# Transposes of two attention steps side by side in every second step

## The chip, the cores and the metric

The kernel runs on one core of a Trainium2 chip. The time is the device time of one execution in microseconds; the number compared is the median over runs. The core's engines run side by side, each through its own list of instructions in order: TensorE (PE in the profile; PEld is its loading of weights), VectorE (DVE), ScalarE (ACT), GpSimd (POOL, hardly used here) and SyncE (SP), which issues the DMAs.

## What is computed

Two layers of an encoder on 512 tokens of 1024 channels. In each layer four token mixers work on one projected input, are gated and summed; an MLP follows. The change touches two of the four, A and C, which have eight query heads and two key and value heads each, of 64 channels. Cut to what matters:

```python
def mixer_a(q, k, v, ...):        # dense: every token sees every token
    sc = einsum('bqhgd,bkhd->bhgqk', qblk, k) * hd ** -0.5
    p = softmax(sc, axis=-1)
    return einsum('bhgqk,bkhd->bqhgd', p, v)

def mixer_c(q, k, v, sink, ...):  # banded: |i - j| <= 128, with a sink logit per head
    sc = where(abs(rel) <= 128, einsum(...) * hd ** -0.5, NEG_INF)
    m = maximum(max(sc, axis=-1), sink)
    p = exp(sc - m)
    l = sum(p) + exp(sink - m)
    o = einsum(p, v) / l
```

## The kernel before

Each matrix is split into a high and a low part (`whi`, `wlo` for weights, `xh`, `xl` for activations), and a product is made of three matmuls per 128 rows, high by high, high by low, low by high (lines 177 to 179). ScalarE makes the high part by a cast (`whi`, L118), VectorE the low part by a subtraction (`wlo`, L127). Weights come by DMA three blocks ahead.

Attention A and then attention C of a layer run through `attn_gqa`. The 512 queries of a head are four tiles of 128, the quarters; a head and a quarter are a **step**, numbered 0 to 31 in an attention (step k is head k//4, quarter k%4). In A a step has four key blocks of 128; in C, where the window is narrow, quarters 0 to 3 have two, three, three and two. The parts of a step, named by a letter:

- `s` scores: two matmuls into a PSUM tile `ps_s` (L796, L797). Two buffers.
- `e` exps: the row's maximum on VectorE (L806 in A, L812 in C), the exponential into `P` on ScalarE (L808 with the sum read after it; L820 and L822 in C). `P` has four buffers.
- `n` norm: the reciprocal of the sum on VectorE (L828), `P` scaled by it on ScalarE (L829).
- `t` transposes: one transpose on TensorE for each key block, from `P` into a PSUM tile `ps_t` (L835). Two buffers.
- `h` high: ScalarE casts `ps_t` into the high half of `PT` (L842). `PT` of a head has one buffer, so the next head's first `h` waits for the values matmuls of the head before.
- `l` low: VectorE subtracts (L845) and by that releases `ps_t`.
- `v` values, only in the fourth quarter: eight matmuls with the transposed probabilities of the whole head (L856); then `o`, `p`, `q` add up and split the output (L863 to L874).

`pipeline` sets the order by hand. It goes through rounds; in round i every entry of a table `ORD` is taken in turn, and an entry such as `t3` means part t of step i - 3. What is written first in a round stands first on its engine. A has the order `v5 t3 h4 n2 e1 o6 l4 s0 q8 p7`; C has `h4 v5 n2 e1 l4 q8 s0 t3 o6 p7`, so its transposes stand at the end of the round, behind the scores. A step's transposes thus stand one round ahead of its `h` and `l`.

`merge` puts other matmul work between the rounds, the **fill**: in A the gates and the projection of mixer B, in C the value projection of mixer D (matmuls of 256 columns, with `vst` copies on ScalarE, L688) and the gates and projection of A. One or two pieces of six matmuls of 512 columns, or twelve of 256, stand between two rounds. The fill's weights are cast on ScalarE and VectorE in the same queues in which the attention's work stands, and its results are taken up there too (L719 to L727).

Of the kernel before, what the change touches and what calls it, by code (L numbers as in the profile page):

```python
# [34 lines left out]

ORD = [[(w[0], int(w[1:])) for w in o.split()] for o in (
    "v5 t3 h4 n2 e1 o6 l4 s0 q8 p7",
    "h4 v5 n2 e1 l4 q8 s0 t3 o6 p7",
)]

MG = ((35, 48, 3), (41, 71, 2), (18, 47, 12))
# [34 lines left out]
class Body:  # L76
# [687 lines left out]
    def attn_gqa(self, l, which, y):  # L764

        nc, ap = self.nc, self.ap
        nv, ns = nc.vector, nc.scalar
        isA = which == 0
        qs = self.qsA if isA else self.qsC
        Kt, Qt, PT, YT = {}, {}, {}, {}  # L770

        def blocks(i):
            return (0, 4) if isA else (max(0, i - 1), min(4, i + 2))
# [11 lines left out]
        def step(h, i):  # L785
            j = h // 4
            b0, b1 = blocks(i)
            n = (b1 - b0) * 128
            st = {}

            def scores():
                if i == 0 and h + 3 < 8:
                    load_q(h + 3)
                ps = st["s"] = self.ps("s")
                qq = Qt[h][:, i * 128:(i + 1) * 128]
                nc.tensor.matmul(ps[:, 0:n], qq, Kt[j][:, 0, b0 * 128:b1 * 128], start=True, stop=False)  # L796
                nc.tensor.matmul(ps[:, 0:n], qq, Kt[j][:, 1, b0 * 128:b1 * 128], start=False, stop=True)  # L797

            def exps():
                ps = st["s"]  # L800
                P = st["P"] = ap.tile([128, S], F32, tag="P", name="P", bufs=4)
                m, nm, ls = self.smt(1, "am"), self.smt(1, "an"), self.smt(1, "al")
                st["l"] = ls
                if isA:
                    rs = self.rqs[:, i, h:h + 1]
                    nv.tensor_reduce(out=m, in_=ps[:, 0:n], axis=AX.X, op=ALU.max, negate=True)  # L806
                    nv.tensor_tensor(out=nm, in0=m, in1=rs, op=ALU.mult)
                    ns.activation(out=P[:, 0:n], in_=ps[:, 0:n], func=AF.Exp, scale=rs, bias=nm, accum_out=ls)  # L808
                else:
                    rs = self.rs8[:, i:i + 1]  # L810
                    mo = C_MC + (b0 - (i - 1)) * 128
                    nv.tensor_tensor_reduce(  # L812
                        out=P[:, 0:n], in0=ps[:, 0:n], in1=self.cs[:, mo:mo + n], scale=1.0, scalar=-3.0e38,
                        op0=ALU.add, op1=ALU.max, accum_out=m,
# [4 lines left out]
                    )  # L819
                    ns.activation(out=P[:, 0:n], in_=P[:, 0:n], func=AF.Exp, scale=rs, bias=nm, accum_out=ls)  # L820
                    e = st["e"] = self.smt(1, "ae")
                    ns.activation(out=e, in_=nm, func=AF.Exp, bias=self.v(l, V_SINK + h), scale=1.0)  # L822

            def norm():
                P, ls = st["P"], st["l"]
                if not isA:
                    nv.tensor_tensor(out=ls, in0=ls, in1=st["e"], op=ALU.add)
                nv.reciprocal(out=ls, in_=ls)  # L828
                ns.activation(out=P[:, 0:n], in_=P[:, 0:n], func=AF.Copy, scale=ls)  # L829

            def transposes():
                P = st.pop("P")
                pt = st["t"] = self.ps("t")
                for b in range(b1 - b0):
                    nc.tensor.transpose(pt[:, b * 128:(b + 1) * 128], P[:, b * 128:(b + 1) * 128], self.ident)  # L835

            def high():
                if i == 0:
# [33 lines left out]
            def out3():  # L872
                if h % 2 == 1:
                    nv.tensor_tensor(  # L874
                        out=y[:, 1, h // 2], in0=YT[h // 2], in1=y[:, 0, h // 2].bitcast(F32), op=ALU.subtract
                    )

            d = dict(s=scores, e=exps, n=norm, t=transposes, h=high, l=low)
            return d | (dict(v=values, o=out1, p=out2, q=out3) if i == 3 else {})

        load_k(0)
# [2 lines left out]
        load_k(1)  # L884
        yield
        steps = [step(h, i) for h in range(8) for i in range(4)]
        yield from self.pipeline(steps, ORD[0 if isA else 1])

# [593 lines left out]
```

## Time and profile before

| | |
|---|---|
| median of 3 runs | 2031.62 us |
| their range | 2030.08 to 2032.27 us |
| the profiled execution | 2030.6 us |
| its span, first to last instruction | 2028.8 us |
| PE busy in the span | 2008.3 us, 99% |
| DVE busy | 1270.8 us, 63% |
| ACT busy | 974.1 us, 48% |
| DMA, mean of the 16 engines | 112 GB/s |

The profile is of one execution. In a row of a timeline stand the start from the span's first instruction and the duration in us, the engine, the line of the code, the operation, the output and the inputs, the shape and how many are merged; in square brackets stands how long the engine was idle before and what ended that. Matmuls overlap each other, and their ends are modelled, so the distance of their starts tells what one costs. Attention A of layer 1 runs from about 208 to 319 us, C from 321 to 437; in layer 2 they are at 1210 to 1322 and 1323 to 1440.

### The profile page before, as it was taken

Reading aid. Unit: us, or ns where it says so; the run is one execution under the profiler, and the core shown is the slowest. Engines: PE = TensorE matmul, PEld = TensorE weight load, DVE = VectorE, ACT = ScalarE, POOL = GpSimd, SP = SyncE. Lnnn points to the kernel's source line nnn. Section 1 sums busy time; section 2 is a strip of 40 time slices with the busy share of each in tenths; the row PEclk is TensorE's granted clock in tenths of the full one; section 3 lists DMA queues with packets and bytes.
Section 4 is the critical chain, followed back from the end, with each engine's and each line's share of the span. In section 5 each row is a group of like instructions: output and inputs, shape, how many; then the busy total and the mean of one; then the engine's idle time right before and its main releaser. Section 6 shows DMA issues by size and latency. Waiting matters only on the chain.

```text
span 2028.8 us, 25698 instructions
## 1 busy us (share of the span) xinstructions
PE 2008.3 (99%) x9752; PEld 1665.0 (82%) x9752; DVE 1270.8 (63%) x2274; ACT 974.1 (48%) x1701; POOL 0.2 (0%) x4
## 2 busy tenths in 40 slices
PE   9999999999999999999999999999999999999998
PEld 7888789887778888888878888898877888888887
DVE  6889775764466544444658897758644665444445
ACT  4357786854534332322323668868445334322322
POOL 0000000000000000000000000000000000000000
PEclk9999999999999999999999999999999999999998
DMA  5454425332134233223335552152421522323231
GB/s 191 136 158 142 130 67 146 116 125 84 53 114 138 94 102 94 96 94 104 123 105 166 156 166 94 62 160 91 135 73 48 173 94 94 104 94 97 94 100 63
DMA packets 87439, 227.03 MB, mean 112 GB/s; under 512 B 15098, under 2 KB 21370, under 8 KB 87316
## 3 DMA queue, kind: packets, MB, share of 16 engines
q1 hardware_dynamic: 84436, 221.20, 34.5%
q10 hardware_dynamic: 2880, 4.20, 0.6%
q8 instruction: 77, 1.26, 0.3%
q14 instruction: 46, 0.38, 0.1%
HBM read 201.08 MB, written 24.27 MB: 111 GB/s over the span
## 4 chain that ended last, share of the span: by engine, by line
PE 89%; DVE 6%; ACT 2%; issue 1%; DMA 1%; SPq 0%; DVEq 0%; ACTq 0%
PE ps_mm L177 13%; PE ps_mm L178 13%; PE ps_mm L179 13%; PE ps_s L177 6%; PE ps_s L178 6%; PE ps_s L179 6%; PE ps_t L177 6%; PE ps_t L179 6%; PE ps_t L178 6%; PE ps_o L856 2%; PE ps_t L835 2%; PE ps_s L796 1%; PE ps_s L797 1%; DVE tt L338 1%; DVE wlo L127 1%
## 5 line engine op out<-in xcount | busy, mean ns | idle before, releaser
L118 ACT CAST whi<-raw 128x1024 fp32r<-128x1024 f32 (+1 forms) x318 | 329.0, 1041 | 334.9 <-PE ps_mm L178 105.6
L127 DVE TENSOR_TENSOR wlo<-raw,whi 128x1024 fp32r<-128x1024 f32 (+1 forms) x318 | 385.0, 1215 | 98.6 <-ACT whi L118 95.6
L177 PE MATMUL ps_mm<-xh,whi 128*128 128x512 f32 x720 | 289.0, 401 | 0.0
L179 PE MATMUL ps_mm<-xh,wlo 128*128 128x512 f32 x720 | 282.6, 392 | 0.0
L178 PE MATMUL ps_mm<-xl,whi 128*128 128x512 f32 x720 | 282.5, 392 | 0.0
L177 PEld LDWEIGHTS ps_mm<-xh,whi 128*128 128x128 f32 x720 | 136.1, 189 | 32.4 <-issue 4.1
L179 PEld LDWEIGHTS ps_mm<-xh,wlo 128*128 128x128 f32 x720 | 135.9, 189 | 29.8
L178 PEld LDWEIGHTS ps_mm<-xl,whi 128*128 128x128 f32 x720 | 136.2, 189 | 26.7
L177 PE MATMUL ps_t<-xh,whi 128*128 128x512 f32 x368 | 143.7, 390 | 0.0
L178 PE MATMUL ps_t<-xl,whi 128*128 128x512 f32 x368 | 143.3, 389 | 0.0
L179 PE MATMUL ps_t<-xh,wlo 128*128 128x512 f32 x368 | 143.2, 389 | 0.0
L177 PE MATMUL ps_s<-xh,whi 128*128 128x512 f32 x352 | 138.6, 394 | 0.0
L179 PE MATMUL ps_s<-xh,wlo 128*128 128x512 f32 x352 | 137.1, 390 | 0.0
L178 PE MATMUL ps_s<-xl,whi 128*128 128x512 f32 x352 | 137.0, 389 | 0.0
L845 DVE TENSOR_TENSOR PT<-ps_t,PT 128x512 fp32r<-128x512 f32 (+2 forms) x128 | 75.1, 587 | 63.9 <-ACT PT L842 54.7
L829 ACT ACTIVATE P<-P,al 128x512 f32<-128x512 f32 (+2 forms) x128 | 82.6, 645 | 17.0 <-DVE al L828 15.7
L719 DVE TENSOR_TENSOR gt<-ps_mm,rb 128x512 f32<-128x512 f32 x54 | 37.2, 688 | 78.3 <-PE ps_mm L179 77.9
L842 ACT CAST PT<-ps_t 128x512 fp32r<-128x512 f32 (+2 forms) x128 | 63.8, 500 | 46.6 <-PE ps_o L856 43.1
L177 PEld LDWEIGHTS ps_t<-xh,whi 128*128 128x128 f32 x368 | 69.1, 188 | 17.3 <-issue 3.0
L179 PEld LDWEIGHTS ps_t<-xh,wlo 128*128 128x128 f32 x368 | 69.1, 188 | 14.3
L178 PEld LDWEIGHTS ps_t<-xl,whi 128*128 128x128 f32 x368 | 69.1, 188 | 14.2
L177 PEld LDWEIGHTS ps_s<-xh,whi 128*128 128x128 f32 x352 | 66.1, 188 | 14.9 <-issue 1.4
(423 smaller groups left out, 4218.2 us busy)
## 6 DMA issues: line engine op xcount, KB each, us to landing
raw<-in_w_dram SPq DMA_DIRECT2D x314, 512.0 KB, 3.5
qsA<-stk SPq DMA_DIRECT2D x32, 128.0 KB, 2.3
qsC<-stk SPq DMA_DIRECT2D x32, 128.0 KB, 2.3
K<-ks SPq DMA_DIRECT2D x16, 256.0 KB, 6.0
Q<-qsA SPq DMA_DIRECT2D x16, 256.0 KB, 3.8
Q<-qsC SPq DMA_DIRECT2D x16, 256.0 KB, 7.0
qD<-stkf SPq DMA_DIRECT2D x24, 128.0 KB, 2.2
kD<-stkf SPq DMA_DIRECT2D x24, 128.0 KB, 2.2
```

The costliest lines, as they stand in the source:

```text
L118: self.nc.scalar.copy(hi[:, s], self.raws[i][:, s])
L127: self.nc.vector.tensor_tensor(out=lo[:, s], in0=raw[:, s], in1=hi[:, s].bitcast(F32), op=ALU.subtract)
L177: mm(ps, sh, mh, start=(k == 0), stop=False)
L178: mm(ps, sh, ml, start=False, stop=False)
L179: mm(ps, sl, mh, start=False, stop=(k == n - 1))
L338: nv.tensor_tensor(out=o, in0=a, in1=b, op=ALU.mult)
L719: nv.tensor_tensor(out=g, in0=ps, in1=self.rb, op=ALU.mult)
L829: ns.activation(out=P[:, 0:n], in_=P[:, 0:n], func=AF.Copy, scale=ls)
L835: nc.tensor.transpose(pt[:, b * 128:(b + 1) * 128], P[:, b * 128:(b + 1) * 128], self.ident)
L842: ns.copy(st["dst"][0], st["src"])
L845: nv.tensor_tensor(out=st["dst"][1], in0=st["src"], in1=st["dst"][0].bitcast(F32), op=ALU.subtract)
L856: nc.tensor.matmul(o, a, b, start=(n_ == 0), stop=(n_ == len(mm) - 1))
```

## The change

Only odd steps have transposes now, and they transpose the step before as well: eight transposes in A, five in C, into the two buffers of `ps_t`. An even step's transposes therefore stand one round later than they did, in the round of its own `h` and `l`. In C the transposes move from the round's end to its front, and `h` behind them.

```diff
 ORD = [[(w[0], int(w[1:])) for w in o.split()] for o in (
     "v5 t3 h4 n2 e1 o6 l4 s0 q8 p7",
-    "h4 v5 n2 e1 l4 q8 s0 t3 o6 p7",
+    "t3 h4 v5 n2 e1 l4 q8 s0 o6 p7",
 )]
...
+            before = (ST.get((h, i - 1)), (blocks(i - 1)[1] - blocks(i - 1)[0]) * 128) if i % 2 else None
+            ST[h, i] = st
...
             def transposes():
-                P = st.pop("P")
-                pt = st["t"] = self.ps("t")
-                for b in range(b1 - b0):
-                    nc.tensor.transpose(pt[:, b * 128:(b + 1) * 128], P[:, b * 128:(b + 1) * 128], self.ident)
+
+                for sb, w in ((before[0], before[1]), (st, n)):
+                    P = sb.pop("P")
+                    pt = sb["t"] = self.ps("t")
+                    for o in range(0, w, 128):
+                        nc.tensor.transpose(pt[:, o:o + 128], P[:, o:o + 128], self.ident)
...
-            d = dict(s=scores, e=exps, n=norm, t=transposes, h=high, l=low)
+            d = dict(s=scores, e=exps, n=norm, h=high, l=low) | (dict(t=transposes) if i % 2 else {})
```

In the changed file the lines stand two to four further down: scores are L798 and L799, transposes L839, `h` L846, `l` L849, values L860.

TensorE in A, at the end of head 0. Before, with the last values matmul, then two rounds; `P_2152` and `P_2178` are steps 5 and 6:

```order
L856 MATMUL ps_o_2203<-PT1_2080,VV_196 128x512
L835 MATMUL ps_t_2212<-cs_77,P_2152 128x128 x4
L796 MATMUL ps_s_2232<-K_1852,Q_1859 128x512
L797 MATMUL ps_s_2232<-K_1852,Q_1859 128x512
...
L835 MATMUL ps_t_2248<-cs_77,P_2178 128x128 x4
L796 MATMUL ps_s_2267<-K_1852,Q_1859 128x512
L797 MATMUL ps_s_2267<-K_1852,Q_1859 128x512
```

The same two rounds in the change:

```order
L860 MATMUL ps_o_2198<-PT1_2080,VV_196 128x512
L839 MATMUL ps_t_2207<-cs_77,P_2114 128x128 x4
L839 MATMUL ps_t_2212<-cs_77,P_2152 128x128 x4
L798 MATMUL ps_s_2232<-K_1852,Q_1859 128x512
L799 MATMUL ps_s_2232<-K_1852,Q_1859 128x512
...
L798 MATMUL ps_s_2262<-K_1852,Q_1859 128x512
L799 MATMUL ps_s_2262<-K_1852,Q_1859 128x512
```

Step 4 (`P_2114`), transposed a round earlier before, has come behind the values matmuls; the next round begins with its scores.

TensorE at the start of C, rounds 3 and 4, with the first fill matmul of each. Before; `P_3197` and `P_3240` are steps 0 and 1:

```order
L796 MATMUL ps_s_3292<-K_3133,Q_3136 128x256
L797 MATMUL ps_s_3292<-K_3133,Q_3136 128x256
L835 MATMUL ps_t_3295<-cs_77,P_3197 128x128 x2
L177 MATMUL ps_mm_3264<-whi_3068,xh_83 128x256
...
L796 MATMUL ps_s_3328<-K_3133,Q_3138 128x256
L797 MATMUL ps_s_3328<-K_3133,Q_3138 128x256
L835 MATMUL ps_t_3331<-cs_77,P_3240 128x128 x3
L177 MATMUL ps_mm_3349<-whi_3145,xh_83 128x256
```

In the change:

```order
L798 MATMUL ps_s_3292<-K_3133,Q_3136 128x256
L799 MATMUL ps_s_3292<-K_3133,Q_3136 128x256
L177 MATMUL ps_mm_3264<-whi_3063,xh_83 128x256
...
L839 MATMUL ps_t_3307<-cs_77,P_3197 128x128 x2
L839 MATMUL ps_t_3310<-cs_77,P_3240 128x128 x3
L798 MATMUL ps_s_3332<-K_3133,Q_3138 128x256
L799 MATMUL ps_s_3332<-K_3133,Q_3138 128x256
L177 MATMUL ps_mm_3349<-whi_3145,xh_83 128x256
```

Step 0 is transposed behind twelve fill matmuls instead of ahead of them, and step 1 ahead of the scores of step 4 instead of behind them.

ScalarE at the same place, round 4, in the change; before, the same operations stand there in the same order:

```order
L846 CAST PT0_3314<-ps_t_3307 128x2x128
L831 ACTIVATE P_3283<-P_3283,al_3286 128x384
L822 ACTIVATE P_3320,al_3323<-P_3320,an_3322,rs8_191 128x256
L824 ACTIVATE ae_3327<-an_3322,ve_78 128x1
L118 CAST whi_3335<-raw_3066 128x1024
L118 CAST whi_3338<-raw_3148 128x1024
```

Nothing moved here: step 0's `h` stands first and two weight casts behind it. What moved is the place on TensorE of the transposes that it reads.

## Rows read from the trace of the kernel before

**Rows 1.** The page, busy time: us, share of the span, instructions.

```profile
PE 2008.3 (99%) x9752; PEld 1665.0 (82%) x9752; DVE 1270.8 (63%) x2274; ACT 974.1 (48%) x1701; POOL 0.2 (0%) x4
```

**Rows 2.** Busy time by stretch, A of both layers; stretch, length, engines, clock, DMA.

```profile
208.00:319.00 111.00, 108.50 (x539) 89.38 (x538) 83.97 (x175) 89.41 (x165) 0.00 (x0) 1.00 0.32 97
1210.00:1322.00 112.00, 110.65 (x541) 91.11 (x542) 83.86 (x176) 89.39 (x165) 0.00 (x0) 0.98 0.31 97
```

**Rows 3.** Timeline of PE, a round of A: start, duration, line, operation, count.

```profile
255.78 0.60 PE L835 MATMUL ps_t<-cs,P 128*128 128x128 f32 x4
256.14 0.48 PE L796 MATMUL ps_s<-K,Q 128*128 128x512 f32 x1
256.46 0.39 PE L797 MATMUL ps_s<-K,Q 128*128 128x512 f32 x1
256.69 0.40 PE L177 MATMUL ps_mm<-yB,whi 128*128 128x512 f32 x1
```

**Rows 4.** Timelines of PE and ACT, start of C in layer 1.

```profile
331.90 0.38 PE L835 MATMUL ps_t<-cs,P 128*128 128x128 f32 x2
333.54 0.28 PE L796 MATMUL ps_s<-K,Q 128*128 128x256 f32 x1
336.46 0.39 PE L178 MATMUL ps_mm<-wlo,xh 128*128 128x256 f32 x1 [0.64 <-DVE wlo L127]
...
332.31 0.37 ACT L842 CAST PT<-ps_t 128x256 fp32r<-128x256 f32 x1
334.12 1.98 ACT L118 CAST whi<-raw 128x1024 fp32r<-128x1024 f32 x2
```

**Rows 5.** Timelines of PE and ACT in A, first step of head 1.

```profile
235.04 0.60 PE L835 MATMUL ps_t<-cs,P 128*128 128x128 f32 x4
...
235.01 0.59 ACT L842 CAST PT<-ps_t 128x512 fp32r<-128x512 f32 x1 [3.26 <-PE ps_o L856]
```

**Rows 6.** The same timelines, end of head 1's scores' wait.

```profile
241.90 0.61 PE L835 MATMUL ps_t<-cs,P 128*128 128x128 f32 x4
242.43 0.50 PE L796 MATMUL ps_s<-K,Q 128*128 128x512 f32 x1
...
242.18 0.19 ACT L808 ACTIVATION_READ_ACCUMULATOR P<-ps_s,an,rqs 128x1 f32 x1
```

**Rows 7.** Timelines of PE and DVE, values matmuls in A.

```profile
258.07 1.32 PE L856 MATMUL ps_o<-PT,VV 128*128 128x512 f32 x5
...
257.33 0.69 DVE L845 TENSOR_TENSOR PT<-ps_t,PT 128x512 fp32r<-128x512 f32 x1 [0.41 <-ACT PT L842]
```

**Rows 8.** Timelines of PE and ACT, scores of step 23 in A.

```profile
280.83 0.48 PE L796 MATMUL ps_s<-K,Q 128*128 128x512 f32 x1
...
280.37 0.19 ACT L808 ACTIVATION_READ_ACCUMULATOR P<-ps_s,an,rqs 128x1 f32 x1
```

**Rows 9.** Timelines of PE, ACT and DVE, head 6 in A.

```profile
302.86 0.60 PE L835 MATMUL ps_t<-cs,P 128*128 128x128 f32 x4
307.44 0.85 PE L856 MATMUL ps_o<-PT,VV 128*128 128x512 f32 x3
...
301.35 0.59 ACT L842 CAST PT<-ps_t 128x512 fp32r<-128x512 f32 x1
303.92 0.62 ACT L870 CAST yA<-yt 128x512 fp32r<-128x512 f32 x1 [0.46 <-DVE yt L868]
...
306.61 0.69 DVE L845 TENSOR_TENSOR PT<-ps_t,PT 128x512 fp32r<-128x512 f32 x1 [1.15 <-ACT PT L842]
```

**Rows 10.** Timelines of ACT, DVE and PE, head 1 in C.

```profile
347.97 0.37 ACT L842 CAST PT<-ps_t 128x256 fp32r<-128x256 f32 x1 [1.97 <-PE ps_o L856]
...
350.60 2.36 DVE L127 TENSOR_TENSOR wlo<-raw,whi 128x1024 fp32r<-128x1024 f32 x2 [1.80 <-ACT whi L118]
353.79 0.55 DVE L845 TENSOR_TENSOR PT<-ps_t,PT 128x384 fp32r<-128x384 f32 x1
...
354.48 0.41 PE L835 MATMUL ps_t<-cs,P 128*128 128x128 f32 x2 [0.24 <-DVE PT L845]
```

More of the change, by code (lines that the diff above doesn't have):

```diff
@@ L769, in attn_gqa @@
         qs = self.qsA if isA else self.qsC
-        Kt, Qt, PT, YT = {}, {}, {}, {}
+        Kt, Qt, PT, YT, ST = {}, {}, {}, {}, {}
         def blocks(i):
```

## The prediction

> **What bounds the kernel now.** I read the page first: the matmul engine is busy 2008.3 of the 2028.8 us [rows 1]. The two attention stretches of layer 1 were cut out with the busy times by stretch: in attention A of layer 1 the matmul engine works 108.5 of 111 us and ScalarE 89.4; in layer 2 it is 110.7 of 112 and 89.4 [rows 2]. So whatever makes TensorE wait goes onto the time in full, and ScalarE, at 80%, is near enough to make it wait. The same windows hold 165 ScalarE and about 540 matmul records in both layers: what is found in layer 1 I count twice.
>
> Then the timelines of single engines, at the rounds where something is late. By "round" I mean one pass of the pipeline loop, by "step k" head k//4, quarter k%4.
>
> **The change part by part.**
>
> *Transposes side by side.* In A a group of four starts at 255.78, the first score matmul follows at 256.14, the second at 256.46, and a plain 512-column matmul takes 0.23 (256.46 to 256.69) [rows 3]. Four last 0.60 and two 0.38 [rows 3, 4], so they start (0.60 - 0.38)/2 = 0.11 apart. The group costs 0.68 - 0.23 = 0.45 against 4 x 0.11 = 0.44. So a group's border costs some 0.01 to 0.02 us; 128 groups become 64 pairs, and 64 borders go: **-0.8 us**, between -0.6 and -1.3. No instruction is removed. The rest of the change is when things happen.
>
> *What is moved.* An even step's transposes (0.44 in A; 0.22 or 0.33 in C, where a step has two or three) leave their round and stand in the next, in front of the odd step's. The orders of ScalarE and VectorE stay as they were. In that next round stands the even step's high copy (ScalarE, line 842), and ScalarE takes its work in order: so far the transposes were a round old when the copy came up, now they are the newest thing TensorE has done. Behind the copy on ScalarE stand the scaling (L829) and the exponentials (L808, L820) of later steps and the weights' `whi` casts (L118); behind those, on VectorE, `low` (L845) and `wlo` (L127); TensorE waits for all of them. Nothing of SP's queue moves. In A the scores of odd steps also come 0.36 earlier (255.78 to 256.14), since no transposes stand before them, and the values matmuls 0.45 earlier.
>
> *A, first step of a head.* The copy at 235.01 had waited 3.26 for the values matmuls, whose last starts 0.23 before the transposes at 235.04, so 0.20 before the copy [rows 5]. Now four transposes come between: 0.23 + 0.33 to the last of them, and 0.30 from there to the copy (in C the second of two transposes starts at 331.90 + 0.11, the copy at 332.31 [rows 4]); less the 0.20, less the 0.45 by which the values come earlier: the copy is **0.2 late** in every head. ScalarE is then busy without a gap until the exponential that ends at 242.37; the scores at 242.43 were already waiting for it (0.53 after the transposes where 0.36 is usual) [rows 6]. In the change they are ready at 241.90 and wait until about 242.64; the second score matmul starts at 242.87 instead of 242.76, and 0.45 of transposes is still to come: **+0.55**.
>
> *Two smaller ones.* The values matmuls at 258.07 need `low`, which ends at 258.02, for their second instruction at 258.30; they will be ready 0.45 earlier, while `low` comes 0.2 later (the delay of the head's first copy, carried along): 0.65 less the 0.27 of slack, **+0.4** [rows 7]. The scores at 280.83 have 0.27 over an exponential that ends at 280.56; they come 0.36 earlier and it comes 0.2 later: **+0.35** [rows 8].
>
> *A, head 6.* The copy of step 26 ran at 301.35. Its transposes now stand in front of those at 302.86, 0.44 before, so the copy can start at about 302.86 - 0.44 + 0.33 + 0.30 = 303.05, 1.7 later. ScalarE has one gap after it, 0.46 before 303.92, so the next copy (306.02) and `low` (ends 307.30) come about 1.25 late, at 308.55. The values at 307.44 want it for their second instruction, at 307.67 - 0.45: **+1.35** [rows 9].
>
> *C, start.* The copy at 332.31 followed its transposes (331.90) at once. Now these stand in front of the round that begins at 333.54; 0.22 less before it, 0.11 to the second, 0.30 to the copy: 333.73, 1.42 late. Four small ScalarE instructions with about 0.2 of slack stand between it and the two `whi` casts at 334.12; these come 1.2 late, and so does `wlo`, for which TensorE was already waiting (0.64 before 336.46) [rows 4]: **+1.2**.
>
> *C, step 7.* The copy at 347.97 had waited 1.97 for the values; they now stand behind the odd step's three transposes, 0.33 later. ScalarE and then VectorE (from 350.60) run without a gap to `low` of step 5, which ends at 354.34 and releases the buffer for which the transposes at 354.48 had waited. All that comes 0.33 later, and the two score matmuls of 384 columns (0.23 x 384/512 = 0.17 each, an estimate) now stand behind these transposes instead of before them: 0.33 + 0.35 = **+0.65** [rows 10].
>
> *Sum.* A 0.55 + 0.4 + 0.35 + 1.35 = 2.65; C 1.2 + 0.65 = 1.85; 4.5 a layer, 9.0 for both, less 0.8: **+8.2 us**. Against the profiled execution (2030.6, span 2028.8) that is 2038.8; the median of the runs shown is 1.0 above it, 2031.6, and 2039.8 is the forecast. What was not priced: other rounds where slack shrinks below 0.1 (more), and heads in which TensorE, once late, no longer outruns ScalarE (less). I put them at half the sum either way: +4 to +14.
>
> One rule speaks against the change on its own. In the trace the granted clock is 1.00, the 2.4 GHz level, in A of layer 1, with its groups of four transposes, and 0.98 in A of layer 2, with the same groups [rows 2]. The Trainium skill ("TensorE: Matmul & The Clock Gate", Part 4: PE-mode transpose) says that a transpose does not count as activity for the clock as other matmuls do. By it, eight in a row might cost clock where four did not; by the row they don't. The sum goes by the row.
>
> **The rivals.**
> 1. *The late copies are absorbed.* ScalarE waits at the copy, but it is idle 20% of A anyway; if the work behind each late copy has more slack than I read, TensorE never sees it. For it: most rounds are like that, only six places a layer were found. Against: at three of the six TensorE already waits for this very chain [rows 4, 6, 10]. It decides if less than half of each delay arrives. Time: 2031.6 - 0.8 = 2030.8, up to 2035 with a part of the waits. This is the one in which the change is not slower.
> 2. *The waits of today vanish.* TensorE's waits at 242.43 (0.17), 336.46 (0.64 or a little more) and 354.48 (0.24 shown) are all that the change could take away: about 1.2 a layer, 2.4, and the 0.8: 2028.4. Against: each is a wait for ScalarE or VectorE, whose work is not cut. A gain over 4 us has no row to come from.
> 3. *The clock falls during pairs.* In A of layer 2, 0.02 of 112 us, 2.2 us, is what a stretch with a lower grant lost [rows 2]. One such in each of the four stretches: 2039.8 + 9 = 2049. Against: the trace shows 1.00 with half the run length.
> 4. *The kernel as built doesn't do it.* The order of instructions shows pairs and unchanged ScalarE and VectorE; I give it nothing.
>
> **How the numbers follow.** About 0.2%, 4 us, is what a measurement of this kernel can tell from no change: faster is below 2027.6, slower above 2035.7. Forecast 0.64 (of it 0.04 so small that it falls within 0.2%); absorbed 0.27, within 0.2%; waits vanish 0.05 (0.03 faster, 0.02 within); clock 0.04, slower. Faster 0.03, same 0.33, slower 0.64. The likeliest time is 2039.8. The range from 2031.5 to 2046.5 leaves out the lower half of the absorbed case with the vanishing waits, and above it the clock and the worst of the forecast, about 0.2 together. The forecast's own range is 2035 to 2046.
>
> **What would show it.** In the profile after: copies of even steps (line 842 before) that wait for transposes, where they waited for the values matmuls or not at all; a wait of about 1.3 at the values matmuls of head 6 in both layers; the wait before `wlo`'s user at the start of C grown from 0.64 to about 1.9; a group of eight lasting 0.88 without a gap in its middle. Wrong would be: TensorE's sum of waits in the two windows as before (rival 1), a gap inside the pairs, or a granted clock under 1.00 around them (rival 3).

## The result and the profile after

The changed kernel takes 2044.4 us in the median of four runs (2040.9, 2042.3, 2046.5, 2046.5), where the kernel before takes 2031.1 beside it: 1.0069 times as long, 95% interval 1.0053 to 1.0085, so between 10.8 and 17.3 us more. The mean granted clock of the four runs is 0.996, 0.995, 0.994 and 0.994 in the same order. The profiled execution is one of the two long ones: 2046.5 us, span 2044.7, which is 15.9 above the span before.

The page's line of busy time, then the windows of the four attention stretches (stretch, length, busy PE, PEld, DVE, ACT, POOL, granted clock, DMA), which answer to [rows 1, 2]:

```profile
PE 2015.3 (99%) x9752; PEld 1666.7 (82%) x9752; DVE 1270.3 (62%) x2274; ACT 973.0 (48%) x1701; POOL 0.2 (0%) x4
```

```profile
210.00:325.00 115.00, 110.69 (x534) 89.73 (x535) 82.61 (x174) 89.50 (x165) 0.00 (x0) 0.99 0.29 90
327.00:440.00 113.00, 110.44 (x700) 100.02 (x699) 77.67 (x231) 84.10 (x203) 0.00 (x0) 1.00 0.36 114
1220.00:1333.00 113.00, 110.06 (x536) 88.92 (x537) 82.13 (x174) 89.29 (x165) 0.00 (x0) 1.00 0.29 92
1335.00:1449.00 114.00, 111.44 (x698) 101.05 (x697) 77.67 (x231) 84.09 (x203) 0.00 (x0) 0.99 0.35 111
```

ScalarE and VectorE are busy as long as before; TensorE's 9752 instructions, as many as before, are busy 7.0 us longer. The list of what TensorE waited for from A's start to C's end of layer 1 (205 to 440 us), first before, then after (total, times, longest):

```profile
PE ps_s L796 <- DVE btq L652: 2.5, 1, 2.5
PE ps_mm L178 <- DVE wlo L127: 0.6, 1, 0.6
PE ps_t L835 <- DVE PT L845: 0.2, 1, 0.2
```

```profile
PE ps_s L798 <- DMA Q<-qsA: 2.8, 1, 2.8
PE ps_mm L178 <- DVE wlo L127: 1.0, 2, 0.9
PE ps_t L839 <- DVE PT L849: 0.7, 1, 0.7
PE ps_s L798 <- ACT P L810: 0.7, 2, 0.5
PE ps_mm L177 <- ACT whi L118: 0.7, 1, 0.7
PE ps_o L860 <- ACT PT L846: 0.7, 1, 0.7
PE ps_o L860 <- DVE PT L849: 0.4, 2, 0.2
```

Lines of the changed kernel stand 2 (scores, exponentials, scaling) or 4 (transposes, copies, values) lower than before. The first row is the wait at A's very first scores, which both have. All the others are new or longer, and each names ScalarE or VectorE. The rows add up to 3.3 us before and 7.0 after; the loss in this stretch is larger, 5.6 (below), because the end of a matmul is modelled and part of what it waits stands in the profile as busy time.

On the page the group of `high` (busy, mean ns | idle before it) read

```profile
L842 ACT CAST PT<-ps_t 128x512 fp32r<-128x512 f32 (+2 forms) x128 | 63.8, 500 | 46.6 <-PE ps_o L856 43.1
```

and those of `low` and `high` now read

```profile
L849 DVE TENSOR_TENSOR PT<-ps_t,PT 128x512 fp32r<-128x512 f32 (+2 forms) x128 | 75.1, 587 | 78.9 <-ACT PT L846 72.9
L846 ACT CAST PT<-ps_t 128x512 fp32r<-128x512 f32 (+2 forms) x128 | 63.6, 500 | 68.2 <-PE ps_t L839 49.5
```

Before, the copies idled 46.6 us, most of it for the values matmuls; now 68.2, most of it for transposes. But waits of an engine that has slack are no loss.

What is lost is read from the **lag**: the start of a score matmul in the changed kernel less its start before, taken at the even steps' scores, which stand just behind a pair. In A both kernels have done the same work there: where the lag is flat nothing is lost; where it rises, TensorE waited or its clock was lower. In C the transposes now stand ahead of a round's scores instead of behind them, so an even step's lag holds 0.13 to 0.25 of transposes that are only moved (two or three of them); there the odd steps are the ones at which the changed kernel has done the same work as before. Worked out from the starts in the two traces of one profile, and in a second profile of the changed kernel (run e10):

| place (lag from step to step) | expected | layer 1 | layer 2 | e10, layers 1, 2 |
|---|---|---|---|---|
| A 10 to 12: scores, head's first copy | 0.55 | 0.59 | 0.60 | 0.59, 0.59 |
| A 14 to 16: values of head 2 | 0.40 | 0.59 | 0.59 | 0.59, 0.59 |
| A 22 to 24: scores of step 23 | 0.35 | 0.51 | 0.48 | 0.48, 0.45 |
| A 26 to 28: not priced | 0 | 0.28 | 0.33 | 0.29, 0.33 |
| A 30 to C 0: values of head 6 | 1.35 | 1.37 | 1.36 | 1.36, 1.36 |
| C 2 to 6: `whi`, `wlo` | 1.20 | 1.33 | 2.83 | 1.33, 2.85 |
| C 6 to 14: transposes for a buffer | 0.65 | 0.69 | 0.71 | 0.69, 0.69 |
| A 6 to C 0, then C 0 to 31 | 2.65, 1.85 | 3.54, 2.05 | 3.66, 3.59 | 3.56, 2.04; 3.53, 3.56 |

Steps 6 and 14 of C hold the same 0.13 of moved work, so the 0.69 between them is lost in full, but of the 1.33 up to step 6 only 1.20 is: at steps 5 and 7 the lag stands 1.20 and 1.19 above step 2. Step 31 is an odd one, so the 2.05 is free of it. The 3.59 of C in layer 2 is the 2.05 of layer 1 and 1.5 of lower clock, of which more below. The attentions so hold 12.8 of the 15.9. The rest of this one profile lies outside the change: 1.8 of waits for weights and queries ahead of A's first scores, falls of the clock of 1.6 each at 213.0 (just behind A's wait for its queries) and 1052.6 us, against which before has one of 1.6 at 1212.8 that is missing here, and some tenths of waits for weights. The second profile, e10, has neither the fall at 213.0 nor that at 1052.6.

Three of these places, by the timelines of the changed kernel. First the head's first copy (start, duration, engine, line, operation, count, wait), which answers to [rows 5, 6]:

```profile
237.85 1.04 PE L839 MATMUL ps_t<-cs,P 128*128 128x128 f32 x8
238.64 0.48 PE L798 MATMUL ps_s<-K,Q 128*128 128x512 f32 x1
...
245.91 0.50 PE L798 MATMUL ps_s<-K,Q 128*128 128x512 f32 x1 [0.49 <-ACT P L810]
...
238.48 0.59 ACT L846 CAST PT<-ps_t 128x512 fp32r<-128x512 f32 x1 [3.60 <-PE ps_t L839]
...
245.66 0.20 ACT L810 ACTIVATION_READ_ACCUMULATOR P<-ps_s,an,rqs 128x1 f32 x1
```

The copy at 238.48 starts in the middle of the pair, when the even step's four are done. From it to the exponential at 245.66 ScalarE runs nearly without a gap, 7.2 us in both kernels, and the scores behind it wait. Then the values of head 6, which answer to [rows 9]:

```profile
307.80 1.03 PE L839 MATMUL ps_t<-cs,P 128*128 128x128 f32 x8
...
313.20 0.50 PE L860 MATMUL ps_o<-PT,VV 128*128 128x512 f32 x1 [0.66 <-ACT PT L846]
313.93 1.43 PE L860 MATMUL ps_o<-PT,VV 128*128 128x512 f32 x5 [0.22 <-DVE PT L849]
...
308.44 0.59 ACT L846 CAST PT<-ps_t 128x512 fp32r<-128x512 f32 x1 [1.43 <-PE ps_t L839]
...
312.59 0.56 ACT L846 CAST PT<-ps_t 128x512 fp32r<-128x512 f32 x1
...
313.18 0.69 DVE L849 TENSOR_TENSOR PT<-ps_t,PT 128x512 fp32r<-128x512 f32 x1 [1.15 <-ACT PT L846]
```

The copy waits 1.43 for its pair, the next one comes at 312.59, `low` waits for that, and the values wait for both. And the start of C, which answers to [rows 4]:

```profile
340.08 0.71 PE L839 MATMUL ps_t<-cs,P 128*128 128x128 f32 x5
...
343.14 0.39 PE L177 MATMUL ps_mm<-whi,xh 128*128 128x256 f32 x1 [0.69 <-ACT whi L118]
344.40 0.39 PE L178 MATMUL ps_mm<-wlo,xh 128*128 128x256 f32 x1 [0.87 <-DVE wlo L127]
...
340.50 0.37 ACT L846 CAST PT<-ps_t 128x256 fp32r<-128x256 f32 x1 [1.49 <-PE ps_t L839]
...
342.06 1.98 ACT L118 CAST whi<-raw 128x1024 fp32r<-128x1024 f32 x2
```

A copy that waits 1.49 stands ahead of the weights' two casts; TensorE, which waited once for the weights before (0.64), waits twice.

### The profile page after: what moved, and what is told of

It reads as the page before. It is cut to its first block, busy times and chain, and to the rows that moved or that the text cites. A ratio compares the mean times of both kernels' runs of the same rounds, so it can differ in the third digit from the quotient of the medians.

```text
span 2044.7 us, 25628 instructions
## 1 busy us (share of the span) xinstructions
PE 2015.3 (99%) x9752; PEld 1666.7 (82%) x9752; DVE 1270.3 (62%) x2274; ACT 973.0 (48%) x1701; POOL 0.2 (0%) x4
## 4 chain that ended last, share of the span: by engine, by line
PE 90%; DVE 4%; ACT 4%; DMA 1%; issue 1%; SPq 0%; DVEq 0%; ACTq 0%
PE ps_mm L177 13%; PE ps_mm L178 13%; PE ps_mm L179 13%; PE ps_t L177 6%; PE ps_t L179 6%; PE ps_t L178 6%; PE ps_s L177 6%; PE ps_s L179 6%; PE ps_s L178 6%; PE ps_o L860 2%; PE ps_t L839 2%; PE ps_s L798 1%; PE ps_o L1007 1%; PE ps_s L799 1%; PE ps_t L981 1%
## 5 line engine op out<-in xcount | busy, mean ns | idle before, releaser
L849 DVE TENSOR_TENSOR PT<-ps_t,PT 128x512 fp32r<-128x512 f32 (+2 forms) x128 | 75.1, 587 | 78.9 <-ACT PT L846 72.9
L846 ACT CAST PT<-ps_t 128x512 fp32r<-128x512 f32 (+2 forms) x128 | 63.6, 500 | 68.2 <-PE ps_t L839 49.5
L831 ACT ACTIVATE P<-P,al 128x512 f32<-128x512 f32 (+2 forms) x128 | 82.7, 646 | 15.8 <-DVE al L830 14.6
```

The source lines that it names most:

```text
L846: ns.copy(st["dst"][0], st["src"])
L849: nv.tensor_tensor(out=st["dst"][1], in0=st["src"], in1=st["dst"][0].bitcast(F32), op=ALU.subtract)
```

## The experiments

Theory L: what costs is that an even step's copy now stands in the round of its own transposes, at a few places. Theory P: eight transposes in a row cost by themselves, at every pair. Theory K: clock and weights outside the attentions. Other rivals are told in the expectations. Times are compared with runs of the kernel before on the same chip, whose median was 2029.1 to 2030.1 there.

**e1, e2: pairs in A only, pairs in C only.** The condition stands where the pair is formed (e1: `isA`; e2: `not isA`); e1 has the old order of C:

```diff
-for sb, w in ((before[0], before[1]), (st, n)):
+for sb, w in ((before[0], before[1]), (st, n)) if isA and i % 2 else ((st, n),):
...
-... | (dict(t=transposes) if i % 2 else {})
+... | (dict(t=transposes) if i % 2 or not isA else {})
```

> Attention C is as before, A as changed. Theory L (late copies: a few places where ScalarE's copy now waits for transposes and TensorE then waits for ScalarE or VectorE): the delay in A of each layer measured in the changed kernel is 3.5 us (in steps of 0.6 at step 12, 0.6 at step 16, 0.5 at step 24, 0.3 at step 28 and 1.4 between step 28 and the start of C), so before + 7.0 = 2038.1 us, and the delay of the score matmuls stays flat through C. Rival P (every pair of eight costs something by itself, evenly): 32 of the 64 pairs, half of the 11 to 13 us, 2037, with a delay that grows evenly from pair to pair. Rival K (clock drops and the weights' waits outside the attentions make most of it): 2031 to 2034.

> Attention A is as before, C as changed. Theory L: in the changed kernel the scores of C lag by a further 1.3 us from step 2 to step 6 and 0.7 from there to step 14, 0.1 more to the end, per layer 2.05; so before + 4.1 = 2035.2 us, with the waits at the start of C for whi and wlo as long as in the changed kernel (0.7 and 0.9 where before had 0.64 for wlo alone). Rival P (even cost of each pair): 2037. Rival K: 2031 to 2034. If a drop of the granted clock follows these waits in one of the layers, 1.7 more.

e1 took 2037.7 against 2030.1 (ratio 1.0037, 1.0024 to 1.0050), e2 2036.2 against 2030.1 (1.0030, 1.0019 to 1.0040). In e1 the lag rises by 3.52 from A's step 8 to C's step 0 in layer 1 and 3.46 in layer 2, in the same steps as in the table, and stays at 2.89 to 2.91 through C of layer 1: 7.0 expected, 7.0 in the trace, 7.6 in the medians. In e2 the lag is flat in A and rises by 2.1 and 3.6 in C; the second holds 1.5 for a clock that falls at 1341.5 us, about 1 us behind the waits for the weights: 4.1 + 1.5 = 5.6, and 6.1 in the medians. The two together are 13.7, as much as the change. Theory P fell: the rise is not even, and A and C don't have the same share. Theory K fell as the main cause: 3.54 + 2.05 + 3.66 + 3.59 = 12.8 of the first profile's 15.9 lie in the attentions.

**e3: all but one pair.** In A the last pair of head 6 is undone (condition `not isA or (h, i // 2) != (6, 1)`).

> The changed kernel, but steps 26 and 27 of A (head 6, its second pair) transposed each in its own round again. Theory L: this one pair in each layer costs 1.37 us through the values matmuls of head 6; without it the time is 2.7 us below the changed kernel, 2041.6 against its median 2044.4, and the lag of the scores from A's step 28 to C's step 0 falls from 1.37 to below 0.2. Rival P: 2 of 64 pairs, 0.35 us less, the step stays above 1.

2039.5 against 2030.1 (1.0045, 1.0030 to 1.0060), 4.9 below the changed kernel's median; the lag from A's step 28 to C's step 0 is 0.25 in layer 1 and 0.32 in layer 2, where it was 1.31 and 1.32. So this pair costs about 1.0 to 1.1 a layer. That agrees with L but for the 0.25 to 0.32 that remain where less than 0.2 was expected: the transposes of step 28 still stand behind head 6's values, which so come earlier, and their second matmul then starts 0.27 late. Its profile has no fall of the clock in C either, 1.5; with twice 1.05 that makes 3.6. Set against the kernel before beside each, 9.4 and 13.3, the two kernels are 3.9 apart.

**e4: copies behind the exponentials.** The thought was that a copy which may not come early can stand later:

```diff
-    "v5 t3 h4 n2 e1 o6 l4 s0 q8 p7",
-    "t3 h4 v5 n2 e1 l4 q8 s0 o6 p7",
+    "v5 t3 n2 e1 h4 o6 l4 s0 q8 p7",
+    "t3 v5 n2 e1 h4 l4 q8 s0 o6 p7",
```

> The changed kernel with its pairs, but in each round ScalarE's and VectorE's work is written in another order: scaling and exponentials (n2, e1) ahead of the high copy (h4), in A and in C. Theory L: the copy no longer stops what stands behind it; scaling and exponentials take 1.4 us, which is longer than the transposes need, so most of the 11 us goes: 2031 to 2036. Rival Q (the copy's own readers set the wait: low, the values and the buffer of the transposes, which all come still later in this order): 2044 or more, up to 2056. Rival P: 2042 to 2044, unchanged.

2130.7, 100 us slower: L's hope for this order was wrong, and Q was right in sign, but its bound, 12 us above the changed kernel, was far too low. Two timelines of e4 in A, VectorE and ScalarE:

```profile
266.74 0.69 DVE L849 TENSOR_TENSOR PT<-ps_t,PT 128x512 fp32r<-128x512 f32 x1 [1.78 <-ACT PT L846]
...
269.08 0.16 DVE L830 RECIPROCAL al<-al 128x1 f32<-128x1 f32 x1
...
265.38 0.76 ACT L810 ACTIVATE P<-ps_s,an,rqs 128x512 f32<-128x512 f32 x1
266.05 0.19 ACT L810 ACTIVATION_READ_ACCUMULATOR P<-ps_s,an,rqs 128x1 f32 x1
266.14 0.57 ACT L846 CAST PT<-ps_t 128x512 fp32r<-128x512 f32 x1
269.33 0.73 ACT L831 ACTIVATE P<-P,al 128x512 f32<-128x512 f32 x1 [2.62 <-DVE al L830]
```

Scaling (L831) waits for the reciprocal (L830), which stands on VectorE behind `low` (L849; in this round a subtraction of the output and one of weights come between), which waits for the copy (L846), which now stands behind the exponential. The two engines no longer work side by side but for long stretches in turn: of A's 32 steps in layer 1, `low` waits 1.3 us or more for the copy in 31, and the scaling waits for the reciprocal in 24, 30 us in all. The copy at the front is what lets VectorE do `low` while ScalarE scales and exponentiates.

**e5: copies one round after their pair.** The other way to give the copy its distance: the even step's `high` and `low` move one round back, beside the odd step's.

```diff
-    "v5 t3 h4 n2 e1 o6 l4 s0 q8 p7",
-    "t3 h4 v5 n2 e1 l4 q8 s0 o6 p7",
+    "v5 t3 H5 h4 n2 e1 o6 L5 l4 s0 q8 p7",
+    "t3 H5 h4 v5 n2 e1 L5 l4 q8 s0 o6 p7",
...
-d = dict(s=scores, e=exps, n=norm, h=high, l=low) | (dict(t=transposes) if i % 2 else {})
+d = dict(s=scores, e=exps, n=norm) | (dict(t=transposes, h=high, l=low) if i % 2 else dict(H=high, L=low))
```

> The changed kernel with all its pairs, but the high and low copies of the even steps stand one round later, together with those of the odd step of the same pair, ahead of scaling and exponentials. Theory L (what costs is that the even step's copy stands in the round of its own transposes): the copies find their transposes a round old again, and the delays of A (3.5 a layer) and C (2.05 a layer) fall by more than half; 2030 to 2036. Rival B (bunching: two copies in one round, 1.0 us of ScalarE at once and 1.1 to 1.4 us of VectorE, make exponentials and casts late in the same way): 2038 to 2045. Rival P (eight transposes in a row cost by themselves): 2042 to 2044.

2027.1 against 2029.3 (0.9991, 0.9982 to 1.0001). All pairs are there and none of the delay: the lag falls from A's step 2 to C's step 0 by 0.94 and 0.61, and through C it ends 0.06 and 0.09 higher. This is the run that decides: P and the bunching are out, L stands. ScalarE's timeline of e5 and what TensorE waited for from A to C in layer 1:

```profile
233.16 1.07 ACT L846 CAST PT<-ps_t 128x512 fp32r<-128x512 f32 x2 [0.93 <-PE ps_t L839]
...
237.88 1.06 ACT L846 CAST PT<-ps_t 128x512 fp32r<-128x512 f32 x2
```

```profile
PE ps_s L798 <- DMA Q<-qsA: 2.7, 1, 2.7
PE ps_mm L178 <- DVE wlo L127: 0.6, 1, 0.6
PE ps_t L839 <- DVE PT L849: 0.5, 1, 0.5
```

Two copies run together, and in A nobody waits for them.

**e6, e7: which pairs.** e6 keeps only the second pair of each head and not head 6's in A (condition `i // 2 and (not isA or h != 6)`); e7 undoes only C's very first pair (`isA or (h, i // 2) != (0, 0)`).

> Of the pairs only the second of each head is kept (quarters 2 and 3), except in head 6 of A; the first two quarters of every head, and head 6's last two, are transposed each in its own round. 31 of 32 pairs minus 17 per attention pair: 15 of 32 a layer stay. Theory L: the copies at the start of a head, which come behind the values matmuls, and that of head 6 make nearly all of the delay, so A keeps at most 0.6 a layer and C at most 0.9: 2030 to 2033 with before at 2030.1. Rival P: half of the pairs, half of the cost, 2036 to 2037.

> The changed kernel without the first pair of C (head 0, quarters 0 and 1), which are transposed each in its own round at the front. Theory L: the waits for whi (0.7) and for wlo (0.9) at the start of C are back at 0.64 for wlo alone, the lag of the scores from C's step 2 to step 6 falls from 1.33 to below 0.2, in both layers: 2.3 to 2.7 us less than the changed kernel, and where the granted clock fell just behind these waits in layer 2, it does not fall there: together 2039 to 2042 against the changed kernel's 2044.4. Rival: the start of C is late for another reason (the transposes' new place in the round), the waits stay: 2042 to 2045.

e6 took 2032.5 against 2029.3 (1.0014, 1.0004 to 1.0023): its lag is flat in A, from -1.70 to -1.82 and from 1.93 to 1.90, and rises by 1.07 and 1.06 in C. Step 28, whose two transposes stand alone here and ahead of step 31's scores, puts 0.14 of moved work into that; at the last head's values matmuls the rise is 0.88 and 0.86, within the 0.9 expected, and 0.68 and 0.67 of it come between steps 6 and 14 (see e8). So the first pairs and head 6's second make all of A's delay, the seven second pairs that A keeps nothing. e7 took 2040.1 against 2029.3 (1.0044, 1.0030 to 1.0059). There the lag from C's step 2 to 6 is 0.14 and 0.12 instead of 1.33 and 2.83, no more than the moved work, and TensorE's only wait at the start of C is the old one:

```profile
339.70 0.38 PE L178 MATMUL ps_mm<-wlo,xh 128*128 128x256 f32 x1 [0.64 <-DVE wlo L127]
```

**e8: C's order without pairs.** No pair anywhere; C's transposes at the front of the round.

> No pairs at all; only the order of C is the changed one, with the transposes at the front of the round instead of behind the scores. Theory L: the transposes come later than they stood at the end of the round before by nothing but what lies between two rounds (the fill), and each copy still stands behind them in the round after; within 0.5 us a layer of before: 2029 to 2031.5 with before at 2030.1. Rival F (the place at the front is what costs in C): the 2.05 us a layer of C come back without a pair, 2034.

2030.8 against 2029.3 (1.0008, 0.9999 to 1.0018). The lag rises by 0.91 and 0.92 in C, of which 0.14 are step 28's moved transposes (at the last head's values it is 0.79 and 0.80): less than half of 2.05, so F fell, but more than the 0.5 that L gave. 0.69 and 0.68 of it come between steps 6 and 14, as in the changed kernel, with this timeline of TensorE in e8:

```profile
353.39 0.41 PE L839 MATMUL ps_t<-cs,P 128*128 128x128 f32 x2 [1.03 <-DVE PT L849]
353.56 0.42 PE L798 MATMUL ps_s<-K,Q 128*128 128x384 f32 x1
```

So this term belongs to the place at the front and not to the pairs: transposes that wait for their buffer there hold up the scores behind them.

**e9: e5 with C's transposes at the end of the round again** (`"H5 h4 v5 n2 e1 L5 l4 q8 s0 t3 o6 p7"`).

> As the run with the copies one round after, but in C the transposes (pairs) stand at the end of the round again, behind the scores, as before. Theory L: that run's last loss, 0.2 us a layer between C's step 6 and step 14 with its wait of 0.5 for the buffer of the transposes, was found without any pair when only the place in the round was changed (0.7), so it belongs to the place; it goes here, and the lag in C falls by 0.2 to 0.6 a layer: 2026.0 to 2027.0 where the run with the copies one round after had 2027.1. Rival: the copies, now only a fill behind their transposes, wait again at the start of C: 2028 to 2030.

2027.7 against 2029.1 (0.9996, 0.9986 to 1.0006). The trace does what L said, the wait for the buffer is gone and the lag falls through C by 0.30 and 0.32; in the medians this drowns among runs from 2025.0 to 2031.8, and 2027.7 lies above the expected 2027.0. Neither e5 nor e9 can be told from the kernel before by the times; the profiled spans, 2024.1 and 2023.1, are 4.7 and 5.7 shorter than before's, but 2.0 and 2.2 of that lie ahead of the first attention and are not theirs.

**e10: the changed kernel again.**

> The changed kernel itself, once more beside the same runs of before. Theory L: before plus 11.1 (2 x 3.5 in A, 2 x 2.05 in C), so 2040 to 2042 where the granted clock does not fall behind the waits at the start of C, with the lag of the scores through the attentions the same as in the first profile to 0.1 us, stage by stage; each fall of the clock adds 1.6. Rival: the attentions' lag itself varies from execution to execution, and 13.3 is right.

2044.3 against 2029.1 (1.0073, 1.0061 to 1.0086). The table shows its lag: the same within 0.03 at every place, and within 0.13 in the sums. So the rival fell, and the profile's 2041.7, span 2040.0, is the lag's sum of 12.7 less 1.7 that it was ahead at the start, and some tenths of weight waits. The median is 2 us above L's bound, which was given for a clock that does not fall. The mean granted clock is 0.996 in the two short executions (2040.1 and 2041.7) and 0.995 in the three long ones (2044.3 to 2045.9); 0.001 of 2040 us is 2 us, so a lower clock goes with the longer times. Where in those executions it fell is not shown.

**The clock at the start of C.** Windows around it, layers 1 and 2, of the changed kernel (first pair of rows), and of e7, which lacks the first pair of C:

```profile
337.00:352.00 15.00, 13.44 (x110) 13.04 (x109) 7.23 (x23) 10.31 (x27) 0.00 (x0) 1.00 0.43 141
1345.00:1360.00 15.00, 13.44 (x97) 13.04 (x96) 6.62 (x20) 8.96 (x23) 0.00 (x0) 0.89 0.47 148
```

```profile
333.00:348.00 15.00, 14.36 (x120) 14.16 (x119) 8.14 (x29) 11.03 (x28) 0.00 (x0) 1.00 0.47 150
1338.00:1353.00 15.00, 14.36 (x119) 14.16 (x118) 8.11 (x27) 11.22 (x28) 0.00 (x0) 1.00 0.47 153
```

The second wait of the changed kernel in layer 2:

```profile
1351.88 0.39 PE L178 MATMUL ps_mm<-wlo,xh 128*128 128x256 f32 x1 [0.88 <-DVE wlo L127]
```

In layer 2 the grant falls to the lower level, at 1353.0, about 1 us behind the waits of 0.69 and 0.88, for some 3 us (0.11 x 15 us at half speed is 3.3), and costs 1.5. Of the profiles that have both waits, the changed kernel, e10 and e2 show this fall in layer 2, e3 doesn't, and none shows it in layer 1; none of the seven that have only the old wait for `wlo` there (before, e1, e5 to e9) shows it in either layer. The waits go with the falls; that they cause them is not shown, and why three of four times and in one layer only stays open.

## Why the prediction was right

**Direction and size.** Slower was forecast, 2039.8 with a range to 2046.5, and 2044.4 came. The forecast was 8.2 above before, the measurement 13.3; the 5 us between them have names.

**The six places** are those where the lag rises. Two terms of A were right to 0.1: the values of head 6 (1.35, measured 1.37) and the first steps of a head (0.55, measured 0.59), and so were C's two (1.2, measured 1.20 without the moved work; 0.65, measured 0.69). The last of them is a cost of the place at the front, as e8 shows without a pair; its two parts, 0.33 and 0.35, add up to 0.68, not to the 0.65 written.

The two smaller ones of A were too small (0.40 and 0.35; 0.59 and 0.51). The copy was as late as forecast (0.23 over TensorE's lag for the first copy of heads 1 to 6); what the terms left out is that the reader starts 0.06 behind what releases it, and that behind such a wait the next matmuls start later still: five values matmuls last 1.43 instead of 1.32, and two scores stand 0.34 apart where 0.23 is usual without transposes before them. For the values, with `low` 0.25 late and 0.22 of slack, that is 0.45 + 0.25 - 0.22 + 0.11 = 0.59. (The 0.36, 0.2 and 0.27 of the other give 0.29, not the 0.35 written.)

One place, A 26 to 28, with 0.3, was among "other rounds where slack shrinks" and not priced: the scores of step 27, which had 0.40 over their exponential before, now start 0.05 behind it. Together 5.6 a layer instead of 4.5: 2.2 of the 5.

**The pairing itself.** The -0.8 did not arrive in the changed kernel, because a small new wait takes the gain back. An odd step's scores come 0.36 earlier, since no transposes stand before them, and so run into ScalarE, which is not earlier. A's step 31 of layer 1, the end of the exponential that frees the scores' buffer, then the two scores:

```profile
310.21 0.20 ACT L810 ACTIVATION_READ_ACCUMULATOR P<-ps_s,an,rqs 128x1 f32 x1
...
310.50 0.45 PE L798 MATMUL ps_s<-K,Q 128*128 128x512 f32 x1
310.79 0.39 PE L799 MATMUL ps_s<-K,Q 128*128 128x512 f32 x1
```

Of the 15 odd steps from 3 on, ten start 0.05 to 0.10 behind that end (before: one), and in all ten the second matmul starts 0.38 to 0.40 behind it, 0.29 to 0.34 behind the first. In the other five the two stand 0.23 apart, as in all 15 of e5. Where the odd step does not wait, the lag falls by 0.05 to 0.06 to the next even one (steps 4 to 6, 18 to 20, 28 to 30 of layer 1); where it waits by 0.06, the lag does not fall (4.60, 4.64 at steps 16 and 18; 4.59, 4.60 at 20 and 22). These waits are too short for the list. So 0.8 of the 5 is a gain that was taken back. With the copies out of the way it is there, and larger than the 0.0125 a pair that was forecast: e9's lag falls by 0.05 to 0.06 from pair to pair in A of layer 1 (-1.42 at step 16, -1.80 at step 30). Where more than 0.01 of that comes from was not followed.

**The clock.** The rival with a falling clock had 0.04 and the wrong cause. The Trainium skill ("TensorE: Matmul & The Clock Gate", Part 4: PE-mode transpose) says that a transpose does not count as busy for the clock in the way other matmuls do; by that, pairs might have cost clock. The trace of e5 shows no such cost: with every pair in place, the window of A in layer 1 shows 1.00:

```profile
208.00:325.00 117.00, 116.16 (x603) 98.53 (x604) 86.54 (x185) 93.75 (x174) 0.00 (x0) 1.00 0.34 102
```

The only fall of its grant near A of layer 2 stands at 1207.7, ahead of the first pair. What goes with lost clock is the two waits that the change makes at the start of C: 1.5, in three of four profiles, in one layer. A place where TensorE begins to wait twice could have been priced with a part of such a fall. With it, 2.2 + 0.8 + 1.5 = 4.5 of the 5 are named.

**The range.** The places were found and priced from rows; the width was not. Half the sum either way, as the text says, is +4.1 to +12.3, and the 13.3 measured lies above that, though its interval reaches down to 10.8; the +14 written has no working behind it. That the time fell inside the range is in part luck: waits at other rounds were named as not priced, the clock at the start of C was not.

**Of the signs,** the copies that wait for transposes, the wait of about 1.3 in front of head 6's values (0.66 and 0.22 in the list; 0.80 + 0.49 = 1.29 by the starts of the two matmuls) and the pair without a gap (eight from 237.85 to 238.64) came as told. The start of C came differently: not one wait grown to 1.9 for `wlo` but 0.69 for `whi` and 0.87 for `wlo`, since the casts themselves now end later than TensorE asks for them. The absorbed case (0.27) fell: nearly the whole of each delay arrives.

## What to carry to other kernels

An instruction that is moved on one engine comes nearer to its reader on the next engine, or farther from it: ask, for every reader, how old its input was when it came up, and if it becomes the newest thing, move the reader by the same round (e5) rather than within its round (e4). Engines that feed each other through such readers keep their overlap by the order on each queue: putting the reader behind independent work cost 100 us here, where its wait had cost 13 with all that came with it. And a stream that comes earlier gains nothing where it meets an engine that has not become earlier (the odd steps' scores). Read the loss from the lag of one landmark instruction between two traces: at points where both kernels have done the same work it rises only where something is lost, and it repeats to 0.1 us a place where run times scatter by 5.

## What the runs showed of the hardware that was not expected

In layer 2 of e2, e10 and the changed kernel the granted clock fell to the lower level about 1 us behind two waits of under a microsecond, 0.69 and 0.87 or 0.88, in a stretch that is otherwise busy, and cost 1.5 us. The same two waits had no fall behind them in layer 2 of e3 and in layer 1 of all four, so they go with the fall and are not enough for it. In e4, with its many waits, the mean grant of A and C's start (210 to 350 us) was 0.93 where it was 1.00 in e5's A, so about 10 us of its 100 (0.07 of 140) are clock in this stretch alone:

```profile
210.00:350.00 140.00, 122.96 (x543) 96.65 (x543) 82.09 (x173) 92.23 (x165) 0.00 (x0) 0.93 0.25 75
```
